# Taps of a causal convolution loaded as fp32 halves and cast by ScalarE, with the start of the program reordered

## The chip, the core and the metric

The kernel runs on one NeuronCore of a Trainium2 chip. The metric is the device time of one execution in microseconds (us); a lower time is better. TensorE (PE) multiplies, VectorE (DVE) and ScalarE (ACT) work on SBUF and PSUM, GpSimd (POOL) and SyncE (SP) issue DMA transfers here. A transfer that POOL issues goes through the software queue (q0 in the profile), one that SP issues through the hardware queue (q1); both run on the same 16 DMA engines.

## What is computed

`x` is 8 x 4096 x 512 and `kernel` is 8 x 512 x 512, both fp32. Each output row is a sum of eight matrix products of the row itself and the seven before it:

```python
def reference(x, kernel):
    B, S, D = x.shape
    K = kernel.shape[0]
    out = np.zeros_like(x)
    for k in range(K):
        if k == 0:
            shifted = x
        else:
            shifted = np.concatenate([np.zeros((B, k, D), dtype=np.float32), x[:, :-k, :]], axis=1)
        out += np.matmul(shifted, kernel[k])
    return out.astype(np.float32)
```

## The kernel before

**Layout.** The 32768 rows of `x` are cut into 128 runs of 256 consecutive rows, one run on each partition; "row t" below is the t-th row of all 128 runs at once, a tile of 128 x 512. TensorE needs such a row transposed, with channels on partitions. Transposed rows live in the ring `XR`, 20 rows in bf16; row t is at place (t + 4) mod 20. One `product` (L115) is four matmuls of 128x128 by 128x512: one row times one 512 x 512 matrix, added up in a PSUM bank. Rows before t = 0 of a run are the last rows of the run on the partition before it; `history` (L290) writes them into `XR` shifted by one column, and VectorE zeroes the column where a sequence starts.

**Two ways of computing.** The first four output rows are computed plainly: 32 products `direct(tap, t)` (L306), eight taps by four rows, collected in the PSUM pairs `pd[0]` (rows 0 and 1) and `pd[1]` (rows 2 and 3). The other 252 rows come in 21 blocks of 12. A block has four nodes, in the order PL, MI, H1, H0, and each works with sums and differences of rows (`Z`, `A`, `S`, `F`, made by VectorE) and with sums and differences of taps. This needs 38 products for 12 rows where the plain way needs 96. Nodes are numbered from 1; node 4 is the first H0 node, a "leaf" with other steps than the rest, for which the actions F0, F1, v0, v1, d0 and d1 do nothing.

**Tap matrices.** `W[a, b, c]` are 512 x 512 in bf16. Eight of them are the taps themselves (a is H0 or H1, b and c are LO or HI): tap k sits where n = 7 - k has the bits a, b, c. The others are 26 sums and differences that VectorE makes, one instruction of 128x2048 each (`wsum` L255, `plus` L266). So the sum PL,HI,HI needs taps 0 and 4, and so on up to the ones that need tap 2. The PL matrices lie in one tile `WP`. Two chunks of it first serve as landing place `H` for the seven history rows, and another as `XF` for the first four rows of `x` in fp32. The places of MI,MID,MID and of MI,MID,HI and MI,MID,LO first hold the rows 0 to 3, 4 to 7 and 8 to 11 of `x` in bf16 (`xin`). 

**The start.** The program fixes the order of instructions on each engine by hand. `fill` (L272) are matmuls on zeros; there are 13 calls of two. Rows 0 to 3 come through SP in fp32 (L383) and are cast by VectorE and ScalarE (L304); they, the history rows and the rows 4 to 11 are transposed on TensorE (`transpose_pe`, L276) and copied to `XR` by ScalarE (`here` L295, `history` L290). Later rows come as bf16 through a DRAM buffer `xd` (`load_x`, L100) and are transposed by a DMA that SP issues (L94).

**The loads.** `load_w` (L251) loads one tap in one transfer on POOL's queue, which casts fp32 to bf16 on its way: 128 partitions x 4 x 512 elements. POOL issues tap 0, the history rows H[4:8], taps 4, 5, 1, 7, 3, 6, then H[1:4], tap 2, the rows 4 to 7, 8 and 9, 10 and 11, and seven `xd` loads. From H[1:4] on, each waits for the eighth transfer before it to have landed, because there are eight semaphores for that queue.

**After the start.** `node_*` functions are the actions of a node: `a1`, `a0`, `u` build a small PSUM pair `q`; ScalarE copies it to the seeds (`s0`, `s1`: L187, L189) and to `DT` (L193); `v` adds a product to a seed; VectorE's `d` (L204, L206) finishes it; `l00` to `l11` add the products with `F` (or `S` for a leaf); `e0`, `e1` combine outputs and store them. `b1` is `a1` of node 4. Actions of nodes 1 to 4 are listed one by one in the order in which they are to run (L473 to L595); from node 5 on (L597) the order is that of `SLOT` (L332). The output tiles `y` have five buffers of 128 x 1024 fp32.

Of the kernel before, what the change touches and what calls it, by code (L numbers as in the profile page):

```python
# [8 lines left out]
LO, HI, MID = 0, 1, 2  # L9
# [5 lines left out]
def kernel(  # L15
# [64 lines left out]
    def tt(o, a, b, op):  # L80
        nc.vector.tensor_tensor(out=o, in0=a, in1=b, op=op)  # L81

    def pair(k):
        return ppool.tile([P, 2, D], f32, name=f"pp{k}")

    def load(o, src):
        nc.gpsimd.dma_start(out=o, in_=src)

    def rows(o, t, n):
        load(o, xr[:, t:t + n, :])  # L90
# [9 lines left out]
    def load_x(t):  # L100
        if t < RUN:
            xd[t] = dpool.tile([P, 4, D], bf, name="xd")
            rows(xd[t], t, 4)
# [43 lines left out]
    def node_A(n):  # L147
        tt(AX[n.k % 2], n.z[:, n.o + 2:n.o + 4], n.z[:, n.o + 3:n.o + 5], ADD)
# [42 lines left out]
    def node_dts(n):  # L191
        if not n.leaf:
            nc.scalar.copy(out=DT, in_=n.q[:, 0])  # L193
# [54 lines left out]
                                       in1=dd[b_], op0=MUL, op1=SUB)  # L248
        store(n.t + 4 + 2 * b_, cc[b_])

    def load_w(tap):  # L251
        n = K - 1 - tap
        load(W[n >> 2, n >> 1 & 1, n & 1], kr[:, :, tap, :])

    def wsum(a, b_, c_):  # L255
        o = W[a, b_, c_]
        if a == MI and b_ != MID and c_ != MID:
            tt(o, W[H0, b_, c_], W[H1, b_, c_], SUB)
        elif b_ == c_ == MID:
            tt(o, W[a, MID, LO], W[a, MID, HI], SUB)  # L260
        elif b_ == MID:
            tt(o, W[a, HI, c_], W[a, LO, c_], SUB)
        else:
            tt(o, W[a, b_, LO], W[a, b_, HI], SUB)

    def plus(*which):  # L266
        for b_, c_ in which:
            tt(W[PL, b_, c_], W[H0, b_, c_], W[H1, b_, c_], ADD)
# [3 lines left out]
    def fill(pw):  # L272
        for h in range(2):
            nc.tensor.matmul(pw[:, h], lhsT=zero[:, 0:P], rhs=zero, start=True, stop=True)  # L274

    def transpose_pe(name, k, src, t0, t1):  # L276
        o = pair(k).bitcast(bf).rearrange("p a (b d) -> p (a b) d", b=2)
        for t in range(t0, t1):
            for c in range(DC):
                nc.tensor.transpose(o[:, t - t0, c * P:(c + 1) * P], src[:, t, c * P:(c + 1) * P],  # L280
                                    ident)
        bank[name] = o[:, 0:t1 - t0]
# [12 lines left out]
    def here(eng, t, name, a, b):  # L295
        eng(out=XR[:, place(t) + a:place(t) + b], in_=bank[name][:, a:b])  # L296

    def load_xin(t, a=0, b=4):
        rows(xin[t][:, a:b], t + a, b - a)
# [3 lines left out]
    def cast(eng, a, b):  # L303
        eng(out=xin[0][:, a:b], in_=XF[:, a:b])  # L304

    def direct(tap, t):  # L306
        n = K - 1 - tap
        product(pd[t // 2][:, t % 2], XR[:, place(t - tap)], W[n >> 2, n >> 1 & 1, n & 1], tap == 0)

    def direct_out(b_):  # L310
        y = y_tile()
        nc.scalar.copy(out=y, in_=pd[b_])
        store(2 * b_, y)

    def seed_plus(b_, c_):
        nc.scalar.copy(out=W[PL, b_, c_], in_=W[H1, b_, c_])

    def seed_minus(b_, c_):
        nc.scalar.mul(out=W[MI, b_, c_], in_=W[H1, b_, c_], mul=-1.0)

    def add_h0(a, b_, c_):
        nc.gpsimd.dma_start(out=W[a, b_, c_], in_=W[H0, b_, c_], accum_op=ADD)

    def z_rows(n, a, b):
        zsum(a, n.t - 3 + a, n.t + 1 + a, b - a, ADD)

    def s_rows(n, a, b):
        tt(SX[n.k % 2][:, a:b], Z[:, a:b], Z[:, a + 2:b + 2], ADD)
# [44 lines left out]
    def go(k, name):  # L373
        there, act = step(k)[name]
        if there:
            act()

    pd = {0: pair(0), 1: pair(1)}
    load_w(0)
    rows(H[:, 4:8], RUN - 4, 4)  # L380
    make_identity(nc, ident)
    nc.vector.memset(zero, 0.0)
    nc.sync.dma_start(out=XF, in_=xr[:, 0:4, :])  # L383
    cast(nc.vector.tensor_copy, 2, 4)
    for k in range(7):
        fill(pair(2 + k % 2))
    go(3, "v1")
    cast(nc.scalar.copy, 0, 2)
    transpose_pe("x0", 2, xin[0], 0, 4)
    load_w(4)  # L390
    here(nc.scalar.copy, 0, "x0", 2, 4)
    go(3, "d0")
    load_w(5)
    load_w(1)
    here(nc.scalar.copy, 0, "x0", 0, 2)
    fill(pair(3))
    load_w(7)
    fill(pair(3))
    direct(0, 3)
    direct(0, 2)  # L400
    fill(pair(2))
    transpose_pe("h4", 3, H, 4, 8)
    history(nc.scalar.copy, -4, "h4")
    load_w(3)
    plus((HI, HI))
    wsum(H1, HI, MID)
    wsum(MI, HI, HI)
    plus((HI, LO))
    wsum(MI, HI, LO)
    direct(0, 1)  # L410
    direct(0, 0)
    direct(4, 3)
    fill(pair(2))
    wsum(PL, HI, MID)
    direct(4, 0)
    direct(4, 2)
    direct(4, 1)
    wsum(H1, MID, LO)
    wsum(MI, HI, MID)
    plus((LO, LO))  # L420
    direct(5, 3)
    wsum(MI, LO, LO)
    wsum(PL, MID, LO)
    load_w(6)
    direct(1, 0)
    rows(H[:, 1:4], RUN - 7, 3)
    direct(1, 3)
    direct(5, 1)
    direct(5, 2)
    direct(1, 1)  # L430
    direct(7, 3)
    direct(1, 2)
    direct(3, 3)
    direct(3, 2)
    direct(3, 0)
    wsum(H0, MID, LO)
    load_w(2)
    load_xin(4)
    wsum(H1, LO, MID)
    wsum(H1, MID, HI)  # L440
    wsum(H1, MID, MID)
    direct(6, 2)
    direct(3, 1)
    transpose_pe("h3", 2, H, 1, 4)
    history(nc.scalar.copy, -7, "h3")
    direct(6, 3)
    load_xin(8, 0, 2)
    direct(2, 2)
    direct(7, 2)
    plus((LO, HI))  # L450
    direct(2, 0)
    transpose_pe("x4", 3, xin[4], 0, 4)
    direct(2, 1)
    direct(7, 0)
    load_xin(8, 2, 4)
    wsum(PL, MID, HI)
    transpose_pe("x8", 2, xin[8], 0, 2)
    here(nc.scalar.copy, 4, "x4", 0, 2)
    here(nc.scalar.copy, 4, "x4", 2, 4)
    fill(pair(3))  # L460
    transpose_pe("x9", 2, xin[8], 2, 4)
    direct(7, 1)
    direct(6, 1)
    wsum(MI, LO, HI)
    direct(5, 0)
    wsum(PL, LO, MID)
    direct(6, 0)
    load_x(12)
    here(nc.scalar.copy, 8, "x8", 0, 2)
    wsum(MI, MID, HI)  # L470
    wsum(PL, MID, MID)
    wsum(MI, LO, MID)
    z_rows(nodes[1], 0, 5)  # L473
    load_x(16)
    node_A(nodes[1])
    here(nc.scalar.copy, 10, "x9", 0, 2)
    z_rows(nodes[1], 5, 7)
    fill(pair(2))
    go(4, "F1")
    direct_out(0)  # L480
    node_a1(nodes[1])
    load_x(20)
    load_x(24)
    s_rows(nodes[1], 0, 3)
    direct(2, 3)
    node_u(nodes[1])
    node_seed(nodes[1], 0)
    node_seed(nodes[1], 1)
    node_a0(nodes[1])
    node_dts(nodes[1])  # L490
    s_rows(nodes[1], 3, 5)
    transpose_x(12)
    node_z(nodes[2])
    node_A(nodes[2])
    node_F(nodes[1], 0)
    node_v(nodes[1], 0)
    node_d(nodes[1], 0)
    go(1, "F1")
    node_v(nodes[1], 1)
    node_d(nodes[1], 1)  # L500
    wsum(MI, MID, LO)
    wsum(MI, MID, MID)
    node_a1(nodes[2])
    direct_out(1)
    go(1, "l00")
    go(1, "s")
    go(1, "l01")
    go(1, "e0")
    go(1, "a0")
    go(1, "dt")  # L510
    go(1, "u")
    go(1, "s0")
    go(1, "z")
    go(1, "F0")
    go(1, "A")
    go(1, "l11")
    go(1, "s1")
    load_x(28)
    go(1, "l10")
    go(1, "v0")  # L520
    load_x(32)
    go(1, "v1")
    go(3, "F0")
    go(1, "d0")
    go(2, "F1")
    go(1, "e1")
    wsum(H0, MID, HI)
    go(1, "a1")
    go(1, "d1")
    go(2, "s")  # L530
    go(2, "l00")
    go(2, "l01")
    go(2, "a0")
    go(3, "v0")
    go(2, "dt")
    go(2, "e0")
    go(2, "z")
    go(2, "u")
    go(2, "s0")
    go(2, "l10")  # L540
    go(2, "s1")
    go(1, "x")
    go(2, "x")
    wsum(H0, MID, MID)
    go(2, "F0")
    go(2, "v0")
    go(2, "d0")
    go(2, "v1")
    go(2, "d1")
    go(2, "a1")  # L550
    go(2, "l11")
    go(2, "A")
    go(3, "l00")
    go(3, "F1")
    go(3, "l01")
    go(3, "u")
    go(2, "e1")
    go(3, "e0")
    go(3, "a0")
    go(3, "s0")  # L560
    go(3, "l10")
    go(3, "s")
    go(3, "z")
    go(3, "A")
    go(3, "l11")
    go(3, "e1")
    go(4, "l01")
    go(3, "s1")
    go(3, "d1")
    go(4, "l00")  # L570
    go(4, "s")
    go(3, "dt")
    go(4, "b1")
    go(4, "l10")
    go(3, "g0")
    go(4, "u")
    go(4, "x")
    go(4, "e0")
    load_x(36)
    go(4, "s0")  # L580
    go(4, "a0")
    go(4, "s1")
    go(4, "F0")
    go(4, "dt")
    go(4, "z")
    go(4, "A")
    go(4, "v0")
    go(4, "l11")
    go(3, "r")
    go(4, "g1")  # L590
    go(4, "v1")
    go(4, "d0")
    go(4, "e1")
    go(4, "a1")
    go(4, "d1")  # L595

    for k in range(5, len(nodes)):  # L597
# [32 lines left out]
```

## Time and profile before

| | |
|---|---|
| time, median of 3 runs (lowest to highest) | 747.08 us (746.89 to 747.51) |
| the profiled execution: its own time | 746.51 us |
| its span, first to last instruction | 744.8 us |
| PE busy | 729.3 us, 98% |
| DVE busy | 697.2 us, 94% |
| ACT busy | 241.3 us, 32% |
| granted TensorE clock, mean | 1.000 |

In a profile, busy time is the union of an engine's instructions; for PE the ends of matmuls are modelled. A group's line reads: start in us, duration in us, engine, source line, operation, what is written and what is read, shape, count, and in brackets how long the engine sat idle before it and what ended that. "DMA share" counts the busy part of the 16 DMA engines (it can exceed 1 a little) and GB/s the bytes they moved, counted at the smaller, bf16, end for a transfer that casts.

PE is busy 98% of the span. Its idle time is 15.5 us (744.8 - 729.3): 7.6 us of it in the first 100 us, 3.1 us in the 620 us from 100 to 720, and 4.8 us in the last 24.8.

### The profile page before, as it was taken

What the parts mean: (1) busy time and instruction counts of PE and PEld (TensorE: products, weight loads), DVE (VectorE), ACT (ScalarE), POOL (GpSimd) and SP (SyncE); (2) the same over time, 40 slices, a digit from 0 to 9 for tenths busy, and PEclk for the clock granted to TensorE, in tenths of its full rate; (3) what the DMA queues carried; (4) which work ended last, traced back from release to release, by engine and by line L of the source; (5) the groups of instructions that cost most, each with busy time, mean ns of one, the idle gap of its engine ahead of it and who ended that gap; (6) DMA issues with size and microseconds to landing.
All of it is one profiled execution on the core that took longest, in us unless ns stands there. A gap on an engine that the chain in (4) does not pass through costs nothing.

```text
span 744.8 us, 8881 instructions
## 1 busy us (share of the span) xinstructions
PE 729.3 (98%) x3354; PEld 331.0 (44%) x3422; DVE 697.2 (94%) x729; ACT 241.3 (32%) x369; POOL 57.8 (8%) x98
## 2 busy tenths in 40 slices
PE   8989999999999999999999999999999999999997
PEld 3444444444444444444444444444444444444443
DVE  2999999999999999999999999999999999999996
ACT  3053233332333333232423333242333323333331
POOL 5200010101010010101011010101101010100000
PEclk9999999999999999999999999999999999999999
DMA  9996859696877969697795969688596968865414
GB/s 199 210 214 161 225 118 251 136 234 162 203 205 163 236 145 235 156 219 182 185 231 138 233 152 236 165 181 239 137 240 142 241 164 188 220 148 179 139 78 170
DMA packets 159372, 138.88 MB, mean 186 GB/s; under 512 B 130144, under 2 KB 134240, under 8 KB 159200
## 3 DMA queue, kind: packets, MB, share of 16 engines
q1 hardware_dynamic: 145456, 99.89, 49.6%
q0 software_dynamic: 13728, 38.15, 28.0%
q8 instruction: 27, 0.44, 0.2%
q10 hardware_dynamic: 144, 0.26, 0.1%
q14 instruction: 17, 0.14, 0.1%
HBM read 77.33 MB, written 99.09 MB: 237 GB/s over the span
## 4 chain that ended last, share of the span: by engine, by line
PE 93%; ACT 1%; issue 1%; DVE 1%; DVEq 0%; ACTq 0%
PE pp L117 92%; ACT pp L187 0%; DVE w L81 0%; PE pp L280 0%; ACT DT L193 0%; ACT XR L296 0%; DVE pp L81 0%; DVE pp L206 0%; DVE y L81 0%; ACT pp L189 0%; DVEq L625 0%; ACT pp L168 0%; ACT pp L171 0%; PE pp L274 0%; DVE F L81 0%
## 5 line engine op out<-in xcount | busy, mean ns | idle before, releaser
L117 PE MATMUL pp<-w,S 128*128 128x512 bf16 x1153 | 269.0, 379 | 1.5
L117 PE MATMUL pp<-w,F 128*128 128x512 bf16 x986 | 248.4, 379 | 1.0
L117 PEld LDWEIGHTS <-S 128*128 128x128 bf16 x1176 | 114.8, 98 | 140.2 <-issue 3.6
L117 PE MATMUL pp<-w,A 128*128 128x512 bf16 x659 | 170.5, 379 | 2.7 <-ACT pp L189 1.2
L81 DVE TENSOR_TENSOR Z<-XR 128x2048 bf16<-128x2048 bf16 (+3 forms) x109 | 154.6, 1437 | 0.1
L117 PEld LDWEIGHTS <-F 128*128 128x128 bf16 x1008 | 98.6, 98 | 119.0
L81 DVE TENSOR_TENSOR S<-Z 128x2560 bf16<-128x2560 bf16 (+1 forms) x85 | 124.8, 1469 | 0.0
L187 ACT COPY pp<-pp 128x512 f32<-128x512 f32 x84 | 57.3, 682 | 158.8 <-PE pp L117 154.0
L117 PEld LDWEIGHTS <-A 128*128 128x128 bf16 x672 | 65.2, 97 | 82.8 <-DVE A L81 4.5
L171 ACT COPY pp<-pp 128x512 f32<-128x512 f32 x63 | 35.9, 570 | 198.9 <-PE pp L117 198.9
L117 PE MATMUL pp<-w,Z 128*128 128x512 bf16 x330 | 85.4, 379 | 1.7 <-ACT DT L193 1.4
L81 DVE TENSOR_TENSOR F<-S 128x1024 bf16<-128x1024 bf16 x126 | 86.6, 687 | 0.0
L106 POOL COPY junk<-A 128x2 bf16<-128x2 bf16 x18 | 17.6, 980 | 557.4 <-DVE A L81 557.4
L232 DVE SCALAR_TENSOR_TENSOR y<-pp,y 128x1024 f32<-128x1024 f32 x42 | 51.3, 1222 | 8.9 <-PE pp L117 8.4
L81 DVE TENSOR_TENSOR A<-Z 128x1024 bf16<-128x1024 bf16 x84 | 57.9, 690 | 1.5
L189 ACT ACTIVATE pp<-pp 128x512 f32<-128x512 f32 x84 | 58.1, 692 | 1.1 <-PE pp L117 1.1
L206 DVE SCALAR_TENSOR_TENSOR pp<-pp,DT 128x512 f32<-128x512 f32 x63 | 43.9, 697 | 14.5 <-PE pp L117 14.5
L229 ACT ACTIVATE y<-pp 128x1024 f32<-128x1024 f32 x42 | 43.1, 1027 | 40.3 <-PE pp L117 40.1
L81 DVE TENSOR_TENSOR y<-y,pp 128x1024 f32<-128x1024 f32 (+1 forms) x43 | 51.1, 1190 | 2.0 <-PE pp L117 1.9
L81 DVE TENSOR_TENSOR y<-pp,y 128x1024 f32<-128x1024 f32 x42 | 51.2, 1219 | 1.7 <-DMA out_dram<-y 1.7
L117 PEld LDWEIGHTS <-Z 128*128 128x128 bf16 x336 | 32.9, 98 | 41.4 <-issue 1.5
L247 DVE SCALAR_TENSOR_TENSOR y<-y 128x1024 f32<-128x1024 f32 x42 | 51.2, 1219 | 0.0
(28 smaller groups left out, 244.9 us busy)
## 6 DMA issues: line engine op xcount, KB each, us to landing
out_dram<-y SPq DMA_DIRECT2D x127, 512.0 KB, 7.7
xd<-in_x_dram POOLq DMA_DIRECT2D x61, 512.0 KB, 10.8
w<-in_kernel_dram POOLq DMA_DIRECT2D x8, 512.0 KB, 15.9
w<-in_x_dram SPq DMA_DIRECT2D x1, 1024.0 KB, 4.9
w<-in_x_dram POOLq DMA_DIRECT2D x2, 512.0 KB, 14.9
XR<-xd SPq DMA_TRANSPOSE x61, 5.4
w<-in_x_dram POOLq DMA_DIRECT2D x2, 256.0 KB, 18.4
w<-in_x_dram POOLq DMA_DIRECT2D x1, 384.0 KB, 20.3
```

The source lines that it names most:

```text
L81: nc.vector.tensor_tensor(out=o, in0=a, in1=b, op=op)
L106: nc.gpsimd.tensor_copy(out=junk, in_=z[:, 0:2])
L117: nc.tensor.matmul(bank, lhsT=comp[:, c * P:(c + 1) * P], rhs=w[:, c, :], start=start and c == 0, stop=c == DC - 1, skip_group_check=True)
L171: nc.scalar.copy(out=n.q[:, 0], in_=n.q[:, 1])
L187: nc.scalar.copy(out=o, in_=q)
L189: nc.scalar.mul(out=o, in_=q, mul=-1.0)
L206: nc.vector.scalar_tensor_tensor(out=p[:, 0], in0=p[:, 1], scalar=-1.0, in1=DT, op0=MUL, op1=SUB)
L229: nc.scalar.mul(out=cc[b_], in_=p, mul=0.5)
L232: nc.vector.scalar_tensor_tensor(out=dd[b_], in0=p, scalar=-0.5, in1=cc[b_], op0=MUL, op1=ADD)
L247: nc.vector.scalar_tensor_tensor(out=cc[b_], in0=cc[b_], scalar=2.0, in1=dd[b_], op0=MUL, op1=SUB)
```

## The change

Taps no longer come through POOL's casting queue. `load_tap(tap, h)` loads one half of a tap (two of its four 128-row chunks) as fp32 through SP into a `y` buffer, of which there are five, and `cast_tap` has ScalarE write that half into the tap's matrix as bf16. There are 16 such loads and 16 such casts. `follow(o, z)` is a ScalarE copy of two elements per partition, from something that was just cast into the place that an `x` load will overwrite; the load must then wait for that copy. So H[4:8] waits for the cast of row 0, the rows 4 to 7 and H[1:4] for the second half of tap 3 (the copies stand behind that cast on ScalarE), and the rows 8 to 11 for its first half. `wsum` is split into two functions without a change of what it does; `wminus` and `wplus` are new and not called. The order of the start and of nodes 1 to 4 is written anew. Nothing is added or removed otherwise: 13 fills, 32 direct products, 26 sums of taps and the actions of the nodes are the same, and from node 5 on the order is that of before.

Cut to what is spoken of later; in the order list only the part up to the first action of node 5 that matters is kept:

```diff
-    def load_w(tap):
+    def tap_w(tap):
         n = K - 1 - tap
-        load(W[n >> 2, n >> 1 & 1, n & 1], kr[:, :, tap, :])
+        return W[n >> 2, n >> 1 & 1, n & 1]
+
+    stage = {}
+
+    def load_tap(tap, h):
+        stage[tap, h] = y_tile()
+        nc.sync.dma_start(out=stage[tap, h], in_=kr[:, 2 * h:2 * h + 2, tap, :])
+
+    def follow(o, z):
+        nc.scalar.copy(out=o[:, 0, 0:2], in_=z[:, 0, 0:2])
+
+    def cast_tap(eng, tap, h):
+        eng(out=tap_w(tap)[:, 2 * h:2 * h + 2], in_=stage[tap, h])
...
     pd = {0: pair(0), 1: pair(1)}
-    load_w(0)
-    rows(H[:, 4:8], RUN - 4, 4)
-    make_identity(nc, ident)
+    nc.sync.dma_start(out=XF, in_=xr[:, 0:4, :])
     nc.vector.memset(zero, 0.0)
-    nc.sync.dma_start(out=XF, in_=xr[:, 0:4, :])
     cast(nc.vector.tensor_copy, 2, 4)
     for k in range(7):
         fill(pair(2 + k % 2))
-    go(3, "v1")
+    load_tap(0, 0)
+    load_tap(0, 1)
+    make_identity(nc, ident)
     cast(nc.scalar.copy, 0, 2)
+    follow(H[:, 4:8], xin[0])
+    rows(H[:, 4:8], RUN - 4, 4)
+    load_tap(4, 1)
+    load_tap(4, 0)
     transpose_pe("x0", 2, xin[0], 0, 4)
...
+    fill(pair(3))
+    cast_tap(nc.scalar.copy, 0, 0)
+    cast_tap(nc.scalar.copy, 0, 1)
+    load_tap(5, 1)
     here(nc.scalar.copy, 0, "x0", 0, 2)
     fill(pair(3))
+    here(nc.scalar.copy, 0, "x0", 2, 4)
+    direct(0, 0)
+    cast_tap(nc.scalar.copy, 4, 1)
     direct(0, 2)
     transpose_pe("h4", 3, H, 4, 8)
     history(nc.scalar.copy, -4, "h4")
+    fill(pair(2))
+    load_tap(5, 0)
+    cast_tap(nc.scalar.copy, 4, 0)
+    load_tap(1, 0)
+    cast_tap(nc.scalar.copy, 5, 1)
     plus((HI, HI))
+    direct(0, 1)
+    cast_tap(nc.scalar.copy, 5, 0)
+    load_tap(1, 1)
+    direct(0, 3)
+    fill(pair(2))
+    cast_tap(nc.scalar.copy, 1, 0)
+    direct(4, 2)
...
+    cast_tap(nc.scalar.copy, 3, 1)
     wsum(H1, MID, LO)
+    follow(xin[4], tap_w(7))
+    wsum(H1, LO, MID)
+    load_tap(3, 0)
+    wsum(H1, MID, MID)
+    load_tap(2, 1)
+    direct(6, 2)
+    follow(H[:, 1:4], tap_w(1))
+    direct(1, 1)
+    cast_tap(nc.scalar.copy, 3, 0)
+    follow(xin[8][:, 2:4], tap_w(3))
+    direct(5, 2)
+    rows(H[:, 1:4], RUN - 7, 3)
...
+    follow(xin[8], tap_w(3))
...
     load_xin(4)
+    transpose_pe("x4", 3, xin[4], 0, 4)
+    load_xin(8, 0, 2)
     history(nc.scalar.copy, -7, "h3")
...
+    transpose_pe("x8", 2, xin[8], 0, 2)
+    go(3, "d1")
+    here(nc.scalar.copy, 4, "x4", 0, 2)
+    wsum(PL, MID, HI)
+    here(nc.scalar.copy, 4, "x4", 2, 4)
+    load_xin(8, 2, 4)
+    direct(6, 1)
+    transpose_pe("x9", 2, xin[8], 2, 4)
     direct(2, 2)
+    wsum(PL, MID, MID)
+    direct(5, 0)
     direct(7, 0)
     fill(pair(3))
     direct(7, 1)
+    here(nc.scalar.copy, 8, "x8", 0, 2)
+    here(nc.scalar.copy, 10, "x9", 0, 2)
+    go(3, "F0")
+    fill(pair(2))
+    z_rows(nodes[1], 0, 5)
+    go(3, "v0")
+    node_A(nodes[1])
+    node_a1(nodes[1])
+    z_rows(nodes[1], 5, 7)
     direct(6, 0)
     wsum(MI, MID, HI)
+    s_rows(nodes[1], 3, 5)
+    s_rows(nodes[1], 0, 3)
+    node_F(nodes[1], 0)
     direct_out(0)
     node_u(nodes[1])
     node_seed(nodes[1], 1)
     node_a0(nodes[1])
+    direct(7, 2)
     node_z(nodes[2])
     node_A(nodes[2])
+    node_seed(nodes[1], 0)
...
```

The order that results on ScalarE's queue at the start is: cast of rows 0 and 1; follow; casts 0a, 0b; `here` rows 0 and 1; `here` rows 2 and 3; cast 4b; `history` of H[4:8]; casts 4a, 5b, 5a, 1a, 1b, 6a, 6b, 7a, 7b, 3b; two follows; cast 3a; two follows; casts 2b, 2a; `history` of H[1:4]; two `here` of rows 4 to 7; two `here` of rows 8 to 11. (0a is the half h = 0 of tap 0, 0b the half h = 1.) On SP's queue the row load comes first, then the 16 half taps in the order 0a, 0b, 4b, 4a, 5b, 5a, 1a, 1b, 6a, 6b, 7a, 7b, 3b, 3a, 2b, 2a, then the two stores of the direct rows, and only then the DMA transposes.

In nodes 1 to 4, four moves matter. Of the sums of taps, MI,MID,HI now comes behind rows 5 and 6 of node 1's `Z` and H0,MID,LO between node 2's `l` products; before, both came ahead of node 1's `Z`. `a0` of node 1 now stands behind seed 1 only. Node 2's `l11` now comes ahead of `b1`. And `a0` of node 4 comes straight behind `b1`.

## The prediction

> **What bounds it.** I read the page first: PE is busy 98%, DVE 94%, at full clock. Then busy time by stage (columns: stage, its length, then busy us and count for PE, PE's weight loads, DVE, ACT, POOL; clock, DMA share, GB/s):
>
> ```profile
> PE 729.3 (98%) x3354; PEld 331.0 (44%) x3422; DVE 697.2 (94%) x729; ACT 241.3 (32%) x369; POOL 57.8 (8%) x98
> ```
>
> ```profile
> 10.00:15.00 5.00, 4.38 (x32) 2.21 (x31) 0.10 (x1) 2.19 (x2) 1.28 (x2) 1.00 1.18 202
> 15.00:20.00 5.00, 4.69 (x22) 2.17 (x23) 4.44 (x5) 0.00 (x0) 1.05 (x2) 1.00 1.24 206
> ...
> 45.00:50.00 5.00, 3.79 (x18) 1.65 (x17) 4.51 (x5) 2.38 (x5) 0.00 (x0) 1.00 1.04 227
> ```
>
> PE's instructions stay the same in number, so time is won or lost only as PE idle time, and the new order ends with node 4 (about 105 us). PE idles 7.6 us in the first 100 us; more cannot be won. The DMA engines are full from 10 us on, DVE from 15 us. The timeline shows what starts the ramp:
>
> ```profile
> 12.74 1.85 ACT L292 COPY XR<-pp 128x2032 bf16<-128x2032 bf16 x1 [2.40 <-PE pp L280]
> ...
> 14.90 1.41 DVE L81 TENSOR_TENSOR w<-w,w 128x2048 bf16<-128x2048 bf16 x1 [8.54 <-DMA w<-in_kernel_dram]
> ...
> 15.31 1.04 PE L117 MATMUL pp<-w,XR 128*128 128x512 bf16 x4 [0.88 <-DVE XR L293]
> ...
> 16.62 13.98 PE L117 MATMUL pp<-w,XR 128*128 128x512 bf16 x63
> ...
> 44.40 1.03 PE L117 MATMUL pp<-w,A 128*128 128x512 bf16 x4
> ...
> 48.38 1.02 PE L117 MATMUL pp<-w,A 128*128 128x512 bf16 x4 [1.21 <-ACT pp L189]
> ```
>
> History rows H[4:8], here called h4, are in `XR` at 14.6 us (12.74 + 1.85), just as tap 4 comes. From then PE and DVE run nearly without a gap until node 1's `a1` at 44.40. These are the times to beat, with two later ones:
>
> ```profile
> 67.37 1.03 PE L117 MATMUL pp<-w,Z 128*128 128x512 bf16 x4
> ...
> 77.73 1.03 PE L117 MATMUL pp<-w,A 128*128 128x512 bf16 x4
> ```
>
> They are `b1` of node 4 and `a1` of node 5, up to which both versions have done the same PE work.
>
> **Skill and trace.** "DMA: Bandwidth & Descriptors", Queues, rings and completion order, says that each DMA engine takes turns between queues packet by packet. The trace agrees: in the DMA view of 50 to 52 us both queues pass 79 packets:
>
> ```profile
> q0 software_dynamic: 79, 0.27, 65.8%
> q1 hardware_dynamic: 79, 0.32, 41.9%
> ```
>
> The same page, SWDGE vs HWDGE vs iDMA, says that only POOL's transfers can cast, so a tap through SP needs the added casts; before has no counterexample. "TensorE: Matmul & The Clock Gate", Part 1, Architectural detail, says that ScalarE takes its instructions strictly in order; ACT's timeline is in program order. This matters: `history` h4 stands ahead of 14 half-tap casts.
>
> **The loads.** Between 3 and 4 us the fp32 row load alone moves 0.43 MB, that is 434 GB/s. POOL's casting loads move 206 GB/s counted in bf16, so 412 in fp32. A tap is 1.05 MB of fp32: 2.4 against 2.5 us. Almost nothing is won by the queue itself; half a tap takes 1.25 us. The row load's first packets come 1.0 us after issue and it landed 0.6 us after its last: half a tap alone takes 2.9 us from issue. With a 1.0 us cast a buffer turns round in about 4 us, five buffers allow 6.2, so DMA, not buffers, sets the pace of the taps.
>
> **h4.** The row load lands at 5.6 as before; its data end at 5.0, and 0a, 0b, 4b follow, landing at 6.9, 8.1, 9.4. ACT: cast 5.6-6.65, follow to 6.85 (0.2, from two-element POOL copies of 0.19). Only now does POOL issue h4; before, it issued at 2.17. In the trace a new POOL transfer sends its first packet 1.0 us after issue when DMA is idle (76.76 to 77.8), but tap 0, issued at 1.26 behind the row load, only at about 4.6, and a store issued at 45.2 at about 48: some 1.8 us more behind another queue's backlog. h4's 8 KB packets then alternate with 2 KB ones, so it gets 80% of the engines and 2.5 us become 3.1. Landing is 6.9 + 1.0 + 3.1 + 0.6 = 11.6 without the backlog's wait, 13.4 with all of it, and 14.4 if turns are equal in bytes and this costs another 1 us. Packets queued ahead are small now; I take 1.0 us of wait: 12.6. Before, h4's transposes began at 11.65.
>
> **ACT and DVE after it.** 16 casts of 1.045 us (the row cast's duration; about 0.95 apart in a row) lie in ACT's idle time except where they wait behind `history`: transposes 12.6-13.65, `history` to 15.55, cast 4a to 16.5. Then 5b 17.45, 5a 18.4, 1a 19.35, 1b 20.3, and as DMA delivers: 6b 22.2, 7b 24.2, 3b 25.5, 3a 26.8, 2a 30.4. DVE's first sum is at 16.55 (before 14.90). It does 20 sums instead of 22 before node 1's `Z`: 24.1 us at 1.13 to 1.25 us a sum, so `Z` starts at 40.65 (before 41.90) and `A` ends at 42.85 (before 44.11), but two sums, 2.3 us, are still owed: DVE is 1.0 us behind.
>
> **PE.** First direct product at 10.05 (before 9.48: casts 0a and 0b stand ahead of `here`). (4,2) at 16.55, then products of 0.853 us (four matmuls of 0.213), one wait of 0.4 us for 1b, and the h3 and x4 transposes come after their data (30.0, 32.6). At 37.3 PE has one thing left, the x9 transposes, which wait for three `here` copies (36.05 to 38.9): 1.65 us idle, against 0.67 before. Three directs, two more and fills: `a1` of node 1 at 43.7. It has one direct product more before it: 43.7 + 0.85 = 44.55 against 44.40, 0.15 late. From there, ACT's direct_out copy (1.02) stands ahead of seed 1, so `a0` waits 0.9 us instead of 1.21. DVE carries the owed sums, so the sum for `b1` ends at 67.6: `b1` at 67.7, PE idle 1.4 us before it; but it has done `l11` already: 67.7 against 67.37 + 0.85, 0.5 early. `a0` of node 4 then waits for ACT's L168: 0.17 (a last matmul of 0.379 runs that far past the next one's slot of 0.213) + 0.58 = 0.8 us with a hand-over, lost, which before was covered by other products. So `a1` of node 5 is at 77.95, against 77.73: 0.2 late. From 80 to 97 DVE has slack of about 1 us (it waits for PE 0.35 us at 96.97 and 0.71 at 101.36), so its lag costs nothing there.
>
> **Loads moved behind.** The rows 4 to 11 land by 35.1, after which seven `xd` loads of 2.5 us end near 53 (before about 54). The transpose of x12 now comes after both stores, at about 50 instead of 45.67, but before it ended at 55.56 because loads starved it; it is needed at 64. No cost; if that cover fails, PE waits for node 4's `Z`.
>
> **Sum.** +0.2 us on the profiled execution's 746.51 (1.7 us of it outside the span): 746.7. The runs' median is 0.57 above that execution: 747.3.
>
> **Rivals.** (1) Slower: ACT's queue is blocked by `history`. Every us that h4 lands after 12.6 moves 4a, DVE's first sum and (4,2) alike. At 13.4, 0.9 later: 748.2; at 14.4: 749.1. It decides from 13.9 on (+1.5). For it: both first-packet delays in the trace; against: the small packets. (2) Faster: h4 lands at 11.6 (-0.7) and DVE is not late for `b1` (-1.4), for instance because sums wait less for casts than I reckoned: 747.3 - 2.1 = 745.2. For it: before hides `b1` completely and the new order does `l11` first; against: DVE's row is full from 15 us on and owes two sums. (3) The change doesn't speed the taps and its buffers slow them: if halves come 1.45 us apart instead of 1.25 from 1b on, 2a is 2.0 us late, less 0.8 slack at (2,0): +1.2, 748.5.
>
> **Numbers.** Forecast (746.0 to 748.6) 0.42; rival 2: 0.31; rival 1, h4 past 13.9: 0.19; rival 3: 0.08, of which 0.03 stays within 0.2%. A change under 0.2% (1.5 us) counts as none, for the measurement cannot tell it well. Faster 0.31, same 0.42 + 0.03 = 0.45, slower 0.19 + 0.05 = 0.24. The range, 744.8 to 749.5, takes in the bounds of h4 and the times of all rivals; the forecast's own is 746.0 to 748.6.
>
> **What would show it.** The new profile should show h4's transposes near 12.6, DVE's first sum near 16.5, sums back to back to 40.7, holes of PE before x9 (1.65), before `b1` (1.4) and after it (0.8). I am wrong if h4 comes past 14, if casts wait for DMA at taps 3 and 2, or if the holes are covered.

## The result, and the profile after

The changed kernel takes 752.3 us (median of 4 runs, 751.59 to 753.14), the kernel before 747.15 (746.89 to 747.51): ratio 1.0068 [1.0056, 1.008], slower by 5.15 us. The forecast was 747.3, its range ended at 749.5.

The profiled execution after has a span of 751.4 us (its own time, 753.14, is 0.8 above the median), before 744.8, so 6.6 us have to be found. First the page's busy times, after:

```profile
PE 730.6 (97%) x3354; PEld 331.2 (44%) x3422; DVE 697.1 (93%) x729; ACT 257.8 (34%) x390; POOL 52.7 (7%) x90
```

As many matmuls and DVE instructions as before; ACT has 16.5 us more, the casts. Where the time went is seen by cutting both spans 645.4 us ahead of their ends (busy time by stage, columns as in the prediction). Before, then after:

```profile
0.00:99.40 99.40, 91.77 (x454) 42.28 (x464) 82.89 (x86) 32.05 (x42) 15.31 (x30) 1.00 0.94 200
99.40:744.80 645.40, 637.49 (x2901) 288.69 (x2959) 614.27 (x644) 209.23 (x328) 42.50 (x68) 1.00 0.76 184
```

```profile
0.00:106.00 106.00, 93.01 (x454) 42.58 (x464) 82.99 (x86) 48.66 (x63) 9.96 (x22) 0.98 0.87 225
106.00:751.40 645.40, 637.54 (x2902) 288.62 (x2959) 614.09 (x644) 209.16 (x328) 42.78 (x68) 1.00 0.75 185
```

The long second parts are alike. The first parts hold the same 454 matmuls, but after needs 6.6 us more for them: PE idles 13.0 us (106.00 - 93.01) instead of 7.6, and is 1.24 us longer busy. Everything happened in the start and nodes 1 to 4. The stages of that part, after:

```profile
10.00:15.00 5.00, 2.13 (x12) 0.81 (x13) 0.00 (x0) 2.27 (x3) 0.00 (x0) 1.00 1.06 302
15.00:20.00 5.00, 4.78 (x28) 2.62 (x27) 1.03 (x2) 3.70 (x4) 0.00 (x0) 0.66 0.60 232
...
30.00:35.00 5.00, 3.43 (x17) 1.47 (x16) 3.92 (x4) 4.54 (x8) 1.70 (x4) 1.00 0.68 208
...
40.00:45.00 5.00, 3.38 (x39) 2.33 (x37) 4.87 (x6) 2.84 (x3) 1.03 (x2) 1.00 1.09 214
```

Four stretches are weak: PE works 3.39 us of the five from 5 on (before 4.77), 2.13 of those from 10 on (4.38), 3.43 of those from 30 on (4.09), 3.38 of those from 40 on (4.88). Beside them the clock falls to 0.66, and the DMA engines, full before (1.18 and 1.24 from 10 to 20), are idle for 40% of 15 to 20. The timeline after names the waits:

```profile
7.01 0.70 POOL L87 DMA_DIRECT2D w<-in_x_dram  x1 [5.70 <-ACT w L262]
...
10.47 1.95 PE L117 MATMUL pp<-w,XR 128*128 128x512 bf16 x8 [1.78 <-ACT XR L316]
...
14.82 1.45 PE L300 MATMUL pp<-ident,w 128*128 128x128 bf16 x16 [2.40 <-DMA w<-in_x_dram]
...
16.30 1.85 ACT L312 COPY XR<-pp 128x2032 bf16<-128x2032 bf16 x1 [4.03 <-PE pp L300]
...
18.05 5.78 ACT L265 CAST w<-y 128x1024 bf16<-128x1024 f32 x6
...
19.13 3.50 DVE L81 TENSOR_TENSOR w<-w,w 128x2048 bf16<-128x2048 bf16 x3 [0.30 <-ACT w L265]
...
25.83 1.04 ACT L265 CAST w<-y 128x1024 bf16<-128x1024 f32 x1 [2.00 <-DMA y<-in_kernel_dram]
...
33.80 3.61 PE L117 MATMUL pp<-w,XR 128*128 128x512 bf16 x16 [1.57 <-ACT w L265]
...
44.70 0.61 PE L300 MATMUL pp<-ident,w 128*128 128x128 bf16 x8 [1.62 <-ACT XR L316]
```

POOL issues h4 at 7.01, as forecast, but its transposes start at 14.82, after 2.40 us of PE idle. ACT idles 4.03 us with its next instruction, `history`, waiting for them, and six casts run only behind it. DVE's first sum is at 19.13, before it was at 14.90. Later ACT itself waits 2.00 us for a half tap, PE 1.57 for a cast, and 1.62 for `here` copies ahead of the x9 transposes. The chain of waits, after, follows the same road (start, duration, what):

```profile
7.01 7.76 DMA w<-in_x_dram
...
16.30 1.85 ACT XR L312
23.85 8.83 DMA y<-in_kernel_dram
...
32.71 1.05 ACT w L265
```

h4's load takes 7.76 us for 1.05 MB of fp32. The DMA view tells why; 12 to 13 us, after:

```profile
q0 software_dynamic: 40, 0.16, 80.5%
q1 hardware_dynamic: 39, 0.07, 20.2%
```

Once both queues move, they pass nearly equal counts of packets and h4 has 80% of the engines, as reckoned. But from 7 to 11 us only q1 moves: q0's first packets come at about 11.0, 4.0 us after issue. And from 19 to 20 us nothing moves at all:

```profile
DMA packets 0, 0.00 MB, mean 0 GB/s; under 512 B 0, under 2 KB 0, under 8 KB 0
```

SP has nothing it may issue: 5a, 1a and 1b went out at 8.16, 9.53 and 12.30, then all five `y` buffers held halves waiting for ACT, and 6a was issued at 19.13, when cast 4a ended. Until 22.91 SP then issued one half per cast, and the second long DMA piece of the chain, 8.83 us up to 3a, begins at 23.85, when the last of the six casts frees a buffer for 3a.

### The profile page after: what moved, and what is told of

Read it like the earlier page. It is cut to its first block, busy times and chain, and to the rows that moved or that the text cites. A ratio compares the mean times of both kernels' runs of the same rounds, so it can differ in the third digit from the quotient of the medians.

```text
span 751.4 us, 8923 instructions
## 1 busy us (share of the span) xinstructions
PE 730.6 (97%) x3354; PEld 331.2 (44%) x3422; DVE 697.1 (93%) x729; ACT 257.8 (34%) x390; POOL 52.7 (7%) x90
## 4 chain that ended last, share of the span: by engine, by line
PE 90%; DVE 3%; DMA 3%; ACT 2%; issue 1%; DVEq 0%; ACTq 0%
PE pp L117 89%; DMA w<-in_x_dram 2%; DMA y<-in_kernel_dram 1%; ACT w L265 1%; DVE w L81 1%; DVE Z L81 1%; PE pp L300 1%; DVE S L81 0%; ACT XR L316 0%; DVE F L81 0%; ACT XR L312 0%; DVE y L81 0%; DVE pp L206 0%; ACT pp L187 0%; ACT pp L168 0%
## 5 line engine op out<-in xcount | busy, mean ns | idle before, releaser
L106 POOL COPY junk<-A 128x2 bf16<-128x2 bf16 x18 | 19.1, 1064 | 557.8 <-DVE A L81 557.8
L206 DVE SCALAR_TENSOR_TENSOR pp<-pp,DT 128x512 f32<-128x512 f32 x63 | 43.6, 692 | 14.3 <-PE pp L117 14.3
```

What stands on the lines that cost most here:

```text
L106: nc.gpsimd.tensor_copy(out=junk, in_=z[:, 0:2])
L206: nc.vector.scalar_tensor_tensor(out=p[:, 0], in0=p[:, 1], scalar=-1.0, in1=DT, op0=MUL, op1=SUB)
```

## The experiments

Each kernel is the changed one with one edit, where nothing else is said. Ratios are against the kernel before, run on the same chip with it; differences from the changed kernel are differences of the medians.

### First: what carries the loss

Theory: h4 is held too long, and ACT's queue stands behind it. Four edits attack this from different sides.

**e1, h4 no longer held.** POOL issues it first.

```diff
     nc.sync.dma_start(out=XF, in_=xr[:, 0:4, :])
+    rows(H[:, 4:8], RUN - 4, 4)
...
-    follow(H[:, 4:8], xin[0])
-    rows(H[:, 4:8], RUN - 4, 4)
```

> The first tiny copy is gone and POOL issues the history rows h4 at once. Theory B (backlog: in the changed kernel h4, issued at 7.0 us, sends no packet before 11.0 because every half tap queued earlier goes first, lands at 14.8, and TensorE, its clock and ScalarE's queue wait for it): h4 lands before 11.8, its transposes start right after the first two direct products near 12, no idle of 2.4 us, no cold clock between 15 and 20 us, 747.5 to 749.0. Theory T (the tap stream through five buffers and ScalarE's casts is what is late, h4 only hides it): tap 3 is still cast at 32 us or later and the time stays above 750.5.

Measured 754.03, ratio 1.0091 [1.0076, 1.0106]: slower still. h4 came as expected, at about 9, but it shared the wire with tap 0, whose half 0a now landed at 9.56 instead of 7.1, and the `here` copies stand behind the casts of 0a and 0b. ACT and PE in its timeline:

```profile
9.56 1.04 ACT L265 CAST w<-y 128x1024 bf16<-128x1024 f32 x1 [2.78 <-DMA y<-in_kernel_dram]
...
11.87 1.92 ACT L316 COPY XR<-pp 128x1024 bf16<-128x1024 bf16 x2
...
12.93 3.60 PE L117 MATMUL pp<-w,XR 128*128 128x512 bf16 x8 [3.95 <-ACT XR L316]
```

The copies of rows that had been transposed long before waited for a tap that they don't need, and PE idled 3.95 us. Then its clock fell to 0.50 (12 to 18 us): the products at 12.93 took 3.60 us instead of 1.95 in the changed kernel, and h4's transposes behind them 1.83 instead of 1.07 at full clock. `history` ran from 18.19 to 20.04, and so ended 1.9 us later than in the changed kernel (18.15). So the late h4 is not the whole cause: with ACT's order kept, a late tap at its head holds up copies that don't need it. The low clock is a rival for part of e1's loss. For these two groups it makes some 1.65 + 0.76 = 2.4 us (an estimate from the durations above), and this run can't part it from the order.

**e2, the half taps 4b, 4a and 5b held too**, each by a tiny copy from row 0 into its buffer.

```diff
-    def load_tap(tap, h):
+    def load_tap(tap, h, hold=None):
         stage[tap, h] = y_tile()
+        if hold is not None:
+            nc.scalar.copy(out=stage[tap, h][:, 0, 0:2], in_=hold[:, 0, 0:2])
...
-    load_tap(4, 1)
-    load_tap(4, 0)
+    load_tap(4, 1, xin[0])
+    load_tap(4, 0, xin[0])
...
-    load_tap(5, 1)
+    load_tap(5, 1, xin[0])
```

> h4 keeps its tiny copy and its issue at 7.0 us; instead the half taps 4b, 4a and 5b are held by tiny copies too, so that only the row load and tap 0 are queued on SP's queue when h4 is issued. Theory B: h4's first packets come when tap 0 is through, near 8, and it lands near 12, 2.8 us earlier than in the changed kernel; 748 to 750. A fixed slow start of POOL's queue (4 us from issue to first packet, whatever is queued) would leave h4 at 14.8 and the time at 752 or above. Theory T: above 750.5.

Measured 751.37, ratio 1.0058 [1.0039, 1.0076]. It missed its purpose: 4b went out at 6.97 and 4a at 7.38, close to h4 (7.16), and q0's first packets still came at 10.3. The 0.9 us to the changed kernel lie within the spread of the runs (750.7 to 752.91).

**e3, `history` behind four casts more**, so that h4's lateness no longer holds up the taps.

```diff
-    history(nc.scalar.copy, -4, "h4")
...
     cast_tap(nc.scalar.copy, 5, 0)
+    history(nc.scalar.copy, -4, "h4")
```

> ScalarE's history copy of h4 and VectorE's memset behind it stand after the casts of taps 4 and 5 instead of before; h4 itself lands at 14.8 as in the changed kernel. Theory B's second part (the copy blocks ScalarE's queue from 12.3 to 18.1 us, so no buffer comes free and DMA stands still from 18 to 20): VectorE's first sum starts near 13.5 instead of 19.1, half tap 6a is issued near 13.5 instead of 19.1, tap 3 is cast by 29 instead of 33.8, the 1.57 us hole at 33.8 closes; 749.5 to 751. If the copy's place doesn't matter: 752 and the tap times unchanged.

Measured 751.20, ratio 1.0052 [1.0035, 1.007]. DVE and PE in its timeline:

```profile
13.47 1.23 DVE L81 TENSOR_TENSOR w<-w,w 128x2048 bf16<-128x2048 bf16 x1 [7.06 <-ACT w L265]
...
15.23 1.07 PE L300 MATMUL pp<-ident,w 128*128 128x128 bf16 x16 [2.60 <-DMA w<-in_x_dram]
...
19.93 15.71 PE L117 MATMUL pp<-w,XR 128*128 128x512 bf16 x71 [1.04 <-DVE XR L313]
```

The first sum is at 13.47, DMA no longer stands still, 3a is cast at 29.55 instead of 33.76, and PE's hole at 33.8 is gone. So the blocked casts, through the buffers that they free, did cause the late taps. But only 1.1 us came back by the medians: PE still waits for h4 (2.60), and then 1.04 for the memset with which DVE zeroes a column behind `history`. DVE's second sum stands behind that memset in its order and starts only at 19.52.

**e4, the low clock.** Five more fills keep PE busy in the wait.

```diff
     direct(0, 2)
+    for _ in range(5):
+        fill(pair(2))
     transpose_pe("h4", 3, H, 4, 8)
```

> Five more calls of fill (ten matmuls on zeros, 2.1 us) stand where TensorE waits for h4, 12.4 to 14.8 us. If the lower clock of 0.66 between 15 and 20 us comes from that idle time, the clock stays at 1.00, the transposes take 1.06 instead of 1.45 us and the eight products after them 1.8 instead of 2.8: 0.8 to 1.4 us faster than the changed kernel, 750.9 to 751.5. If the clock falls for another reason or is hidden by later waits, no change: 752.3.

Measured 752.13, ratio 1.0064 [1.0046, 1.0083], runs from 751.05 to 753.09: no gain that the runs can tell. The mean clock is 0.999 (0.996 in the changed kernel), yet the products with tap 4 wait all the same, for ACT's cast of 4a:

```profile
19.32 7.50 PE L117 MATMUL pp<-w,XR 128*128 128x512 bf16 x33 [0.30 <-ACT w L265]
```

In the changed kernel these products start at 19.98, 0.9 us after that cast ended, because the matmuls ahead of them ran slowly. At full clock they are 0.66 us earlier and wait for the cast instead. Whether these 0.66 us reach the end of the program is not shown: the interval leaves room for about 1 us either way.

### Second: h4's first packet, and the rest of the program

**e5, nothing but 0a and 0b ahead of h4.** With e2's `hold`, 4b, 4a and 5b now wait for the `here` of rows 2 and 3.

```diff
-    load_tap(4, 1)
-    load_tap(4, 0)
...
-    load_tap(5, 1)
...
     here(nc.scalar.copy, 0, "x0", 2, 4)
+    load_tap(4, 1, XR[:, place(2):place(2) + 1])
+    load_tap(4, 0, XR[:, place(2):place(2) + 1])
+    load_tap(5, 1, XR[:, place(2):place(2) + 1])
```

> The half taps 4b, 4a and 5b are held by tiny copies behind the two copies of rows 0 to 3 (about 11.4 us), so that after tap 0 nothing is queued on SP's queue when h4 is issued at 7.1. If h4's late start comes from the transfers queued or being queued beside it, its first packets come by 8.6 and it lands by 11.7 (in the changed kernel 11.0 and 14.8); if POOL's queue needs 3.4 to 4.1 us in any case, 10.5 and 13.5 or later. h4 is then in XR some 1.7 us earlier but taps 4 and 5 are on the wire later: 750.0 to 751.3.

**e6, as e5, but 4b queued as in the changed kernel**; only 4a and 5b are held.

> As the run with 4b, 4a and 5b held, but 4b is queued from the start, so one half tap (1.3 us of DMA time) stands ahead of h4 beyond tap 0. If h4 waits for exactly what is queued ahead, first packets near 9.2 us and landing near 12.3. If any busy hardware queue costs the same 3.4 to 4.1 us, first packets at 10.5 or later.

e5: 752.21, ratio 1.0077 [1.0062, 1.0092]. e6, a single run: 751.49. In e5 h4's first packets came 1.4 us after its issue at 7.31 and its transposes ran at 12.38, without a wait. But tap 4 then came late. PE, e5:

```profile
12.38 1.07 PE L302 MATMUL pp<-ident,w 128*128 128x128 bf16 x16
...
19.39 12.49 PE L117 MATMUL pp<-w,XR 128*128 128x512 bf16 x55 [3.35 <-ACT w L267]
```

What PE no longer waited for h4 (2.40) it waited for the cast of tap 4 (3.35). The held halves went out only at 11.50, and from 8 to 13 us the DMA engines moved 0.05 to 0.21 MB each us, against 0.39 in the changed kernel from 9 to 11: holding them left the wire partly empty. Together with e2 and the changed kernel this gives the first-packet delay of h4 against what SP had queued ahead of it (0a had been moved by then):

| kernel | queued ahead | POOL issues | first packets | delay |
|---|---|---|---|---|
| e5 | 0b | 7.31 | 8.70 | 1.4 |
| e6 | 0b, 4b | 7.24 | 8.71 | 1.5 |
| e2 | 0b, 4b (4a 0.2 us after h4) | 7.16 | 10.28 | 3.1 |
| changed | 0b, 4b, 4a, 5b | 7.01 | 11.04 | 4.0 |

The delay is not a fixed 4 us, and it is longest with the longest backlog, but it doesn't grow by the same step for each half tap: 4b adds only 0.1 us from e5 to e6. What lies closest, by the bytes that q1 had moved, is the end of the loads ahead. In e5 the wire was empty from 7.7 us on, so the 1.4 us are start-up alone. In e6 and e2 4b's data were through at 8.96 and 9.98, within 0.3 us of h4's first packets. In the changed kernel 4a's were through at 10.11, and h4 began while 5b moved. So h4 was served roughly after what stood ahead of it; an exact rule is not shown. In e6 h4 then moved slowly at first and landed at 14.3, later than expected.

**e7, the kernel before with the changed order from node 1's `Z` on.** Loads, taps and order up to there are those of before, apart from two sums and the direct products that the new order does later.

```diff
-    direct(6, 0)
-    load_x(12)
...
-    wsum(MI, MID, HI)
...
     z_rows(nodes[1], 0, 5)
...
+    z_rows(nodes[1], 5, 7)
+    direct(6, 0)
+    wsum(MI, MID, HI)
...
```

> The kernel before, with its loads and its start, but from node 1's Z on in the order of the changed kernel (and with the sums MI,MID,HI and H0,MID,LO and the direct products that this order does later left for later). Theory N (the new order of nodes 1 to 4 costs time by itself: holes before and after b1, 1.4 us more than before from a1 of node 1 to b1 and 0.9 us more to a1 of node 5): 748.5 to 749.8. If the node order only passes on the late start: 747.0 within 0.6.

Measured 746.43, ratio 0.9997 [0.9989, 1.0006]: the new order of nodes 1 to 4 costs nothing that the runs can tell. The two holes are there, in PE's timeline of e7:

```profile
67.78 1.02 PE L117 MATMUL pp<-w,Z 128*128 128x512 bf16 x4 [0.63 <-DVE w L81]
...
69.53 1.89 PE L117 MATMUL pp<-w,A 128*128 128x512 bf16 x8 [0.73 <-ACT pp L168]
```

In the sum with the other waits there they cost nothing. What is lost is lost ahead of node 1.

**e8, the taps through SP and ACT kept, everything around them put right.** h4 is issued first (as in e1), the `here` copies and h4's transposes come ahead of the casts of tap 0, two products come ahead of the x9 transposes, and from node 1's `d0` on the order is that of before (that part is not printed).

```diff
     nc.sync.dma_start(out=XF, in_=xr[:, 0:4, :])
+    rows(H[:, 4:8], RUN - 4, 4)
...
-    follow(H[:, 4:8], xin[0])
-    rows(H[:, 4:8], RUN - 4, 4)
...
-    fill(pair(3))
-    cast_tap(nc.scalar.copy, 0, 0)
-    cast_tap(nc.scalar.copy, 0, 1)
     load_tap(5, 1)
     here(nc.scalar.copy, 0, "x0", 0, 2)
-    fill(pair(3))
     here(nc.scalar.copy, 0, "x0", 2, 4)
+    fill(pair(3))
+    transpose_pe("h4", 3, H, 4, 8)
+    fill(pair(2))
+    cast_tap(nc.scalar.copy, 0, 0)
+    cast_tap(nc.scalar.copy, 0, 1)
+    history(nc.scalar.copy, -4, "h4")
     direct(0, 0)
...
-    transpose_pe("h4", 3, H, 4, 8)
-    history(nc.scalar.copy, -4, "h4")
...
-    transpose_pe("x9", 2, xin[8], 2, 4)
     direct(2, 2)
     wsum(PL, MID, MID)
     direct(5, 0)
+    transpose_pe("x9", 2, xin[8], 2, 4)
...
```

> A version against the causes found: POOL issues h4 first and nothing holds it; the copies of rows 0 to 3 and the transposes of h4 stand ahead of the casts of tap 0; two direct products cover the wait for the x9 transposes; from node 1's d0 on the order of before. Taps still come as fp32 halves through SP. If the causes are those (h4 behind the queued taps, ScalarE's order, node order), history is in XR by 14 us, tap 4 is cast by 16, TensorE has no hole over 1 us until node 1: 745.5 to 748.0. If the tap stream by itself is too slow (theory T), taps 7 and 3 are late again, 749.5 or more.

Measured 747.06, ratio 1.0002 [0.9994, 1.0011]: the whole loss is gone, with all 16 half-tap loads and casts still there. ACT, DVE and PE in its timeline:

```profile
12.27 1.86 ACT L312 COPY XR<-pp 128x2032 bf16<-128x2032 bf16 x1
...
16.05 3.50 DVE L81 TENSOR_TENSOR w<-w,w 128x2048 bf16<-128x2048 bf16 x3 [1.24 <-ACT w L265]
...
28.61 1.04 ACT L265 CAST w<-y 128x1024 bf16<-128x1024 f32 x1
...
29.70 3.61 PE L117 MATMUL pp<-w,XR 128*128 128x512 bf16 x16 [1.15 <-ACT w L265]
...
42.85 0.69 DVE L81 TENSOR_TENSOR A<-Z 128x1024 bf16<-128x1024 bf16 x1
43.60 1.04 PE L117 MATMUL pp<-w,A 128*128 128x512 bf16 x4
```

`history` ends at 14.13, 4.0 us earlier than in the changed kernel, and behind it the casts free buffers in time: the DMA engines move 0.37 to 0.41 MB each us from 9 to 27, and the cast of 3a ends at 29.65 instead of 33.76. A last hole for tap 3 (1.15) costs little, because `a1` of node 1 then waits for `A`: it starts as soon as DVE has made it.

### Third: which parts of e8 carry it

**e9, only the x9 transposes moved** behind (2,2) and (5,0), as in the last lines of e8's diff.

> Only the x9 transposes move: the direct products (2,2) and (5,0) stand ahead of them and cover TensorE's 1.62 us hole at 44.7. If TensorE's own holes add up to the loss, 750.6 to 751.2. If VectorE's full row (from 31 us on it has no gap until node 1's Z and A) sets when node 1 starts, TensorE only waits elsewhere: 752.3 within 0.6.

**e10, only e8's head**: the diff of e8 without the x9 lines, and with the changed order of nodes 1 to 4.

> Of the version at the pace of before, only the head: h4 issued first by POOL, the copies of rows 0 to 3 and h4's transposes ahead of the casts of tap 0; the x9 transposes and the order of nodes 1 to 4 are those of the changed kernel. If the head carries the whole loss: 746.5 to 748.0. If the x9 hole or the node order matter too: 748.5 or more.

**e11, only ACT's order at the head**; h4 stays held by the tiny copy.

```diff
-    cast_tap(nc.scalar.copy, 0, 0)
-    cast_tap(nc.scalar.copy, 0, 1)
     load_tap(5, 1)
     here(nc.scalar.copy, 0, "x0", 0, 2)
     fill(pair(3))
     here(nc.scalar.copy, 0, "x0", 2, 4)
+    cast_tap(nc.scalar.copy, 0, 0)
+    cast_tap(nc.scalar.copy, 0, 1)
     direct(0, 0)
```

> Only ScalarE's order: the copies of rows 0 to 3 stand ahead of the casts of tap 0, h4 is still held and issued at 7.0 us. With h4 issued first alone at 754.0 and both together (the head only) as forecast at 746.5 to 748.0, this is the fourth corner. If both are needed (h4 still lands at 14.8 and blocks ScalarE): 751.5 to 752.6. If ScalarE's order is the cause by itself: below 749.5.

| | us | ratio | against the changed kernel's 752.3 |
|---|---|---|---|
| e9 | 750.68 | 1.0048 [1.0031, 1.0064] | -1.62 |
| e10 | 748.84 | 1.0025 [1.0015, 1.0036] | -3.46 |
| e11 | 751.81 | 1.0066 [1.0051, 1.0081] | -0.5 |

e9's gain is the hole itself. The end of the start, `a1` of node 5, in PE's timeline of the changed kernel and of e9:

```profile
84.30 1.03 PE L117 MATMUL pp<-w,A 128*128 128x512 bf16 x4
```

```profile
82.59 1.03 PE L117 MATMUL pp<-w,A 128*128 128x512 bf16 x4
```

1.71 us earlier, for a hole of 1.62: PE, not DVE, held the program there. e10's head is no full cure, for the x9 hole stays. Its PE timeline:

```profile
9.62 1.07 PE L300 MATMUL pp<-ident,w 128*128 128x128 bf16 x16 [1.54 <-DMA w<-in_x_dram]
...
40.27 0.61 PE L300 MATMUL pp<-ident,w 128*128 128x128 bf16 x8 [1.62 <-ACT XR L316]
```

Set beside e1 and e11: h4 early alone +1.7 (e1, its low clock included), ACT's order alone -0.5 (e11, within the spread of its runs, 751.6 to 752.5), both -3.46 (e10). e10 has a third edit, h4's transposes and `history` ahead of the first product, which was not tried alone. Neither of the first two gains anything that the runs can tell without the rest: with h4 late the reordered ACT queue still stands before `history`, and with the old order an early h4 delays tap 0 and so the `here` copies.

**e14, head and x9 together**, that is e10 and e9, to see whether the two add up.

> The head and the moved x9 transposes together, with the changed kernel's own order of nodes 1 to 4. If the loss is the sum of the two (3.46 and 1.62 us, each measured alone against the changed kernel's 752.3) and the node order is neutral: 752.3 - 5.1 = 747.2, that is, no difference from before. If they overlap, 747.8 or more; if the node order is a gain once the start is on time, 746.5 or less.

Measured 747.23, ratio 1.0011 [1.0003, 1.002] (the kernel before, run beside it, took 746.31). 752.3 - 3.46 - 1.62 is 747.22, so by the medians they add up. That the two figures agree so closely is partly luck: the kernel before was 0.84 us faster here than beside the changed kernel, so against it e14 is still 0.8 us (0.2 to 1.5) slower. Reckoned by ratios instead, the gains of e9 and e10 leave 1.0005, within e14's interval. Neither e8 nor e14 is faster than the kernel before.

## Why the prediction was wrong

**The step that failed is the landing of h4: "Packets queued ahead are small now; I take 1.0 us of wait: 12.6".** It put the first packet 2.0 us after issue, 1.0 for an idle wire and 1.0 of wait. Measured were 4.0: first packet at 11.04, landing at 14.8, past the upper bound of 14.4 and past the 14 that was named as a sign of being wrong. The bounds for the wait, nothing to 1.8 us, came from two transfers in the trace of before that were read inexactly. A POOL load on an idle wire took 1.2 us from issue to its first packet (76.76 to 77.98); tap 0 took 3.6 (1.26 to 4.87, not 4.6), and the store, which SP had issued, 3.4 (45.2 to 48.61). Behind a backlog that is up to 2.4 us more, and the upper landing would have been 6.9 + 3.6 + 3.1 + 0.6 = 14.2 (an estimate), near the measured one. To take little of this wait for the sake of small packets was the error. In the table of e5, e6, e2 and the changed kernel the packets ahead are of one size, yet the delay runs from 1.4 to 4.0 us with what SP had been given before. Packet size then entered as reckoned, but later: 80% share, and 3.1 us of data forecast for 3.2 measured (11.0 to about 14.2, where q0's last full packets are).

The Trainium skill's page "DMA: Bandwidth & Descriptors", Latency and other measured facts, gives about 1 us to the first byte of such a transfer. On an idle wire the trace is a little above it (1.2 before, 1.4 in e5); with a backlog it was 4.0, and the measurement decides. The turn-taking by packets of that page's section Queues, rings and completion order fits once both move in the changed kernel (40 against 39 packets), but doesn't explain the wait before the first one, and in e11 the counts were far from equal (see the end).

**What followed, by the prediction's own rule.** "Every us that h4 lands after 12.6 moves 4a, DVE's first sum and (4,2) alike" held for the first two: h4 was 2.2 late, its transposes 0.4 longer at the low clock, and the cast of 4a ended at 19.1 instead of 16.5 and the first sum came at 19.13 instead of 16.55, both 2.6 late. (4,2) came at 19.98, 3.4 late, because the matmuls ahead of it ran at the low clock too. By h4's lateness alone the time would have been about 749.5 to 750 (an estimate).

**The second step that failed: "DMA, not buffers, sets the pace of the taps".** It holds as long as ACT casts when a half lands: e8 keeps the wire full from 9 to 27 us with the same five buffers. But ACT stood 4.03 us at `history`, the five buffers were full, and the wire was empty from 18 to 20 us. Tap 3 was complete at 33.76 where I had 26.8. About 4.1 us of that are the stall, for in e8 and e3, without it, 3a's cast ends at 29.65 and 29.55. The other 2.8 are the pace itself: in e8 most casts come 1.35 us or more apart instead of 1.25, and 7b's waits 1.62 us for its load. The turnaround of a buffer, put at about 4 us, was mis-sized too: a half takes about 7 us from issue to landing, in e8 (median 7.0) as in the changed kernel (7.4). I had the block of ACT as rival 1 and slow buffers as rival 3 and priced them as separate; here the first caused the second. That added the hole of 1.57 us at 33.80, so that (4,2) 3.4 late and this hole make 5.0 of the 5.8 us by which `a1` of node 1 missed its 43.7 (49.46).

**The x9 hole: "1.65 us idle, against 0.67 before".** Right: 1.62, and by the medians e9 (1.62) and e14 against e10 (1.61) give just that back. In the sum it was to be balanced by an otherwise equal start; when the start was late, it came on top.

**Smaller steps.** "Almost nothing is won by the queue itself" is right (e8). The two owed sums were to leave 1.4 us ahead of `b1`: 0.63, and over nodes 1 to 4 no loss (e7, where `b1` came at 67.78 for a forecast of 67.7). The wait of 0.8 us behind `b1` was 0.73, that ahead of `a0` of node 1 0.83 for 0.9. I hadn't foreseen the clock of 0.66; e4 shows no gain from avoiding it. It does break "time is won or lost only as PE idle time": 1.24 of the 6.6 us are longer busy time. I had rival 2 (faster) at more than the rival that came true, for which both first-packet delays in the trace of before had spoken.

**The balance.** 5.15 us lost: 3.46 are the head (h4 behind the queue, ACT in order, and the tap stream that stalls on both), 1.62 the x9 transposes; 0.07 is left. The parts are differences of medians, each uncertain by some tenths, and e14 against its own kernel before leaves 0.2 to 1.5 us unaccounted. e8, which has the node order of before as well, leaves nothing clear of the noise. The difference between e14 and e8 is too small to say whether the node order has a part in it.

## What to carry to other kernels

A transfer on one queue that is made to wait for an event need not start at that event: here its first packet came 1.4 to 4.0 us after issue, later where the other queue had been given more in the meantime. So look in the trace for what is queued ahead, and don't price the wait by the packets' size. On an engine that works in order, put no instruction that waits for a late transfer ahead of copies that free staging buffers: the loads behind them stop, and here one load that came two us later than forecast made the last half of tap 3 four us later than it came without the stall. When two edits at one place are to be judged, try them together as well: here one alone lost 1.7 us, the other changed nothing that the runs can tell, and both, with a third small move, gained 3.5.

## What was unexpected in the hardware

- h4's first packet came 1.4, 1.5, 3.1 and 4.0 us after its issue in e5, e6, e2 and the changed kernel, the later the more SP had queued. One reading is that a transfer gets behind what is queued when it is issued. e11 speaks for it the other way round: h4 was issued at 7.36, two more halves at 10.89 and 11.83, and from 12 to 14 us h4 passed 102 packets against 27 of q1, which had full speed again only when h4 was through. But it doesn't fit everything: in e1, e8, e10 and e14 h4 was issued at about 1.25, behind the row load and 0a. It began at 5.4 to 5.5, 4.1 to 4.3 us after issue, when the row load had gone (4.8 to 5.0) but 0a had not. A start of some 4 us behind a busy hardware queue would fit these and the changed kernel (and e3, e4, e9 and e11, with the same halves ahead: 4.0 to 4.1), but not e5, e6 and e2. The rule is open.
- A transfer through POOL also starts slowly: in e5 h4 moved 0.14 MB between 8.7 and 10 us, alone on the wire, and 0.21 in the next us. The `xd` load that POOL issued at 76.76 of before moved 0.13 MB between 78 and 79.
- From 22 to 25 us, after, the hardware queue moved only 0.23 to 0.29 MB each us with its engines about 95% busy, against 0.37 to 0.41 in e8 from 9 to 27. The same shows in e2 from 8 to 10 us (0.23 and 0.30) and in e5 from 13 to 15 (0.26 and 0.29). All three come shortly after the wire had run empty in part. The cause is open.
- PE's clock fell to 0.66 in the stage from 15 to 20 us after holes of 1.78 and 2.40 us with 1.95 us of work between. The Trainium skill's page "TensorE: Matmul & The Clock Gate", What's actually happening, puts such a drop down to an idle window of about 3.4 us; no single hole here was that long, and five more fills in the second one (e4) prevented it. The length of a hole alone doesn't decide in these runs: after one of 3.35 us in e5 the clock stayed at 1.00, after one of 1.88 in e11 it fell to 0.50.
